# Differential attention first, with plain fp32 scores on row tiles and PV of two units on column tiles

## The chip, the cores and the metric

One core of one Trainium2 chip runs the whole program. The metric is device time in microseconds (us), from launch to the end of the program; the span is the part of it that the profiler sees the engines in. TensorE (PE) multiplies matrices, VectorE (DVE), ScalarE (ACT) and GpSimd (POOL) work on the rest, and SyncE (SP) issues most of the transfers.

## The reference

Two layers of a diffusion trunk on 640 tokens (512 latent ones on a grid of 8 rows of 64, and 128 context ones), width 1024. A layer projects the modulated, normalised tokens once and splits the columns into four groups of 256: three kinds of attention with four heads of 64 each, and a convolution. Their outputs go through one projection, and a feed-forward part of width 4096 follows. The latent tokens also read 128 cached keys.

```
# differential attention: two maps of 32 columns a head, both rotated by rope
p = softmax(q1 @ k1.T * scale) - lam * softmax(q2 @ k2.T * scale)
o_da = rmsnorm(p @ v) * g * (1 - lam_init)
# neighbourhood attention: 8 rows x 16 columns around the token, with a bias, and the context
p = softmax(concat(qg @ kb.T * scale + bias, q @ kc.T * scale)); o_na = p @ v
# latent attention (MLA): 64 + 32 columns a head, queries and keys out of low-rank projections
o_mla = softmax(concat(q_nope, q_rope) @ k_m.T * scale) @ v_m
# convolution over 31 tokens for each channel, layernorm, silu
mixed = concat(o_da, o_mla, o_na, o_conv) @ w_out
x = x + g1 * mixed;  x = x + g2 * (relu(h @ w_ff1)**2 @ w_ff2)
```

## The kernel before

Tokens lie along the free dimension, channels along the 128 partitions. A product of projections is made of three fp32r matmuls (`mm3`, lines 244 to 246): activations and weights are each cut into a high and a low part, and high x high, high x low and low x high are summed. The weights come in granules of 512 KB through a ring; ScalarE rounds the high part (L192) and POOL, or now and then VectorE, subtracts it (L193).

A layer's mixer (`mix`) runs in this order: the convolution's projection; values for neighbourhood and MLA tiles (`in_v`); four column tiles (`mtile`) of queries and keys, at this place those of the neighbourhood heads; the differential values and the rotated key of MLA with its transposes (kr, L582); then `pipeline`, in which 60 units of attention (a head with 128 queries) go through the stages of the string `PROGRAM`, one unit started in each step. "Sa0 ... T2 ... PV3" says that a unit's scores are issued in its own step, the transposes of its probabilities two steps later and the product with the values (PV) three steps later. Units come in three blocks of 20: neighbourhood, differential, MLA. The stages: S is the scores on TensorE, m the maximum on VectorE, x the exponential on ScalarE, sc the scaling (for the differential heads the combine of two maps, L883), T five transposes on TensorE (L686), ev the copy out of PSUM, PV L697, oc the copy or cut of the output. While units run, `plan` puts pieces of projections between them as fillers, each with a first and a last step out of the table `PL`: first `rest()`, the queries and keys of the differential heads and MLA's first projections.

The differential scores before are single-pass: `da_cut` cuts the scaled queries and the keys (32 columns a map) into high and low parts, `da_stack` copies them by DMA (L842, L843) into a stack of four blocks of 32 partitions, and one fp32r matmul over 128 partitions gives the sum of four products (L863 for the 128 context queries, L865 and L866 for 512 and 128 keys). Neighbourhood scores are fp32 matmuls on 64 partitions (L756 to L758). PV multiplies by the 128 columns of two heads, and half of the output is used.

Beside that the 60 taps of the convolution (L423) run on VectorE in the background; behind them POOL adds two channels (L438), in POOL's one queue with the cuts of granules. `rope` is a shuffle and a product on VectorE (L488, L489) and a product and a sum on POOL (L490, L491). The engines take their instructions in the order that a scheduler writes down when the program is built.

PSUM has three slots of 1024 columns for scores and transposes (`slot`) and two banks of 512 (`g`) for pieces and outputs.

Of the kernel before, what the change touches and what calls it, by code (L numbers as in the profile page):

```python
# [16 lines left out]
T = 640  # L17
# [42 lines left out]
DR = 2  # L60
CUT = "DDDDDGDD"
LEADM = (3, 6, 6, 7)
PL = (0, 15, 22, 24, 27, 26, 34, 34, 41, 46, 59, 25, 28, 58, 63, 18, 23)
# [12 lines left out]
CB = "DDDD"  # L76
# [3 lines left out]
PROGRAM = "Sa0 ma0 | T2 ev2 xa0 Sb0 mb0 xb0 sc1 | PV3 oc3 |".split()  # L80


class Builder:
# [347 lines left out]
    def conv_finish(self, l, dst):  # L431
# [23 lines left out]
        r = [self.F("e", 6144, 512), self.A("cr", 0, 128)]  # L455
# [154 lines left out]
    def da_evac(self, l, p, kind):  # L610
        nc = self.nc

        def evac(h, ps):
            t0, t1 = HALF[h]
            dst = self.qk_q("da", p) if kind == "q" else self.qk_k("da", p)
            nl = min(t1, NLAT) - t0
            if t1 > NLAT:
                c0 = 512 if kind == "q" else 640
                nc.scalar.copy(dst[:, c0:c0 + 128], ps[:, nl:t1 - t0])
                if kind == "k":  # L620
                    nc.sync.dma_start(self.d["dak"][l, :, p], dst[:, 640:768])
            self.rope(dst[:, t0:t0 + nl], ps[:, 0:nl], t0, nl)
        return evac
# [23 lines left out]
    def in_mla(self, l):  # L647
# [31 lines left out]
        self.da_cut(0)  # L679
        self.chain(self.da_stacks(0))  # L680
# [13 lines left out]
    def pv(self, u, p, vals):  # L694
        u["o"] = self.g()[:, 0:128]
        for b, v in enumerate(vals):
            self.nc.tensor.matmul(u["o"], v[:, p * 128:p * 128 + 128] if v.shape[1] > 128 else v, u["pt"][:, b * 128:b * 128 + 128],  # L697
                                  start=b == 0, stop=b == len(vals) - 1)

    def o_copy(self, u, h, i, row):  # L700
        r = slice(64 * (h % 2), 64 * (h % 2) + 64)
        self.nc.scalar.copy(row[r, i * 128:i * 128 + 128], u["o"][r])

    def o_split(self, u, h, i):
        r, c = slice(64 * (h % 2), 64 * (h % 2) + 64), slice(i * 128, i * 128 + 128)
        hi, lo = (self.R("ob", off, 2, T)[r, h // 2, c] for off in (0, 5120))
        self.split(hi, lo, u["o"][r], self.nc.vector)
# [22 lines left out]
    def na_bias(self, kind):  # L730
        return self.F("e", 8192 + 1536 * kind, 384)

    def na_bias_load(self, l, h, kind):
        self.nc.sync.dma_start(self.na_bias(kind), self.d["nab"][l, h, kind])

    def na_unit(self, l, h, i, orow):
        nc = self.nc
        p, r0 = h // 2, 64 * (h % 2)
        rows = slice(r0, r0 + 64)
        q = self.qk_q("na", p)[rows, i * 128:i * 128 + 128]  # L740
        k = self.qk_k("na", p)[rows]
        v = self.v("na")
        nk = 128 if i == 4 else 384
        u = {"nb": nk // 128}

        def S():
            sl = self.slot()
            u["s_"], u["t"] = sl[:, 0:nk], sl[:, 640:1024]
            if i == 4:
                nc.tensor.matmul(sl[:, 0:128], q, k[:, 640:768], start=True, stop=True)  # L750
                return
# [3 lines left out]
            pair = k[:, lo:lo + 2 * step].rearrange("p (a b) -> p a b", b=step)[:, ::-1 if prv < nxt else 1, 0:64]  # L755
            nc.tensor.matmul(sl[:, 0:128], q, pair, start=True, stop=True)  # L756
            nc.tensor.matmul(sl[:, 128:256], q, k[:, i * 128:i * 128 + 128], start=True, stop=True)
            nc.tensor.matmul(sl[:, 256:384], q, k[:, 512:640], start=True, stop=True)  # L758

        def mx():  # L760
# [3 lines left out]
            else:  # L764
                kind = (0, 1, 1, 2)[i]
                nc.vector.tensor_tensor_reduce(out=u["s_"], in0=u["s_"], in1=self.na_bias(kind), scale=-1.0,
                                               scalar=3e38, op0=ALU.add, op1=ALU.min, accum_out=m)
                if i != 1 and h < 3:
                    self.na_bias_load(l, h + 1, kind)

        def ex():
            s = u["s"] = self.small()
            u["e"] = self.F("e", 1536 * ((h * 5 + i) % 4), nk)
# [5 lines left out]
            "PV": lambda: self.pv(u, p, [v[:, 5]] if i == 4 else [self.edge(p)[:, i], v[:, i], v[:, 4]]),  # L779
            "oc": lambda: self.o_split(u, h, i),  # L780
        }

    def mla_unit(self, l, h, i, orow):
        nc = self.nc
        q = self.mq[0:96, h, i * 128:i * 128 + 128]
        k = self.mk[0:96, h]
        v = self.v("na")
        nk = 128 if i == 4 else T
        u = {"nb": nk // 128}

# [13 lines left out]
        def ex():  # L804
# [7 lines left out]
            "PV": lambda: self.pv(u, h // 2, [v[:, 5]] if i == 4 else [v[:, j] for j in range(5)]),  # L812
            "oc": lambda: self.o_split(u, h, i),
        }

    def stk(self, mm):
        return self.R("h", 5632 * mm, T), self.R("h", 5632 * mm + 2560, KEYS)

    def da_hl(self):
        return [self.R("h", 22528 + o, n) for o, n in ((0, T), (2560, T), (5120, KEYS), (8192, KEYS))]  # L820

    def da_cut(self, p):
        nc = self.nc
        qh, ql, kh, kl = self.da_hl()
        q, k = self.qk_q("da", p), self.qk_k("da", p)
        nc.scalar.activation(qh, q, AF.Copy, scale=DA_SCALE)
        nc.vector.scalar_tensor_tensor(out=ql, in0=q, scalar=DA_SCALE, in1=qh.bitcast(F32), op0=ALU.mult, op1=ALU.subtract)
        self.split(kh, kl, k)

    def da_stacks(self, p):  # L830
        for par in range(2):
            yield from self.da_stack(p, par)

    def da_stack(self, p, par):
        nc = self.nc
        qh, ql, kh, kl = (a.bitcast(F32) for a in self.da_hl())
        for mm in (2 * par, 2 * par + 1):
            rows = slice(32 * mm, 32 * mm + 32)
            sq, sk = (a.bitcast(F32) for a in self.stk(mm))
            for b in range(4):  # L840
                to = slice(32 * b, 32 * b + 32)
                nc.sync.dma_start(sq[to], (qh, qh, ql, ql)[b][rows])  # L842
                nc.sync.dma_start(sk[to], (kh, kl, kh, kl)[b][rows])  # L843
                if b % 2:
                    yield

    def da_unit(self, l, h, i, orow):
        nc = self.nc
        v = self.v("da")
        st = [self.stk(2 * (h % 2) + c) for c in range(2)]  # L850
        nk = 128 if i == 4 else T
        sq = self.F("sq", 40 * (h // 2 % 2), 5, 2)
        u = {"nb": nk // 128}

        def S(c):
            if c == 0:
                u["sl"] = [self.slot(), self.slot()]
                u["t"] = self.slot()
                u["s"], u["ee"] = self.small(2), [self.etile(nk), self.etile(nk)]
            sl, (q, k) = u["sl"][c], st[c]  # L860
            q = q[:, i * 128:i * 128 + 128]
            if i == 4:
                nc.tensor.matmul(sl[:, 0:128], q, k[:, 640:768], start=True, stop=True)  # L863
            else:
                nc.tensor.matmul(sl[:, 0:512], q, k[:, 0:512], start=True, stop=True)  # L865
                nc.tensor.matmul(sl[:, 512:640], q, k[:, 512:640], start=True, stop=True)  # L866
# [8 lines left out]
        def sc():  # L875
# [12 lines left out]
            "Sa": lambda: S(0), "Sb": lambda: S(1), "ma": lambda: mx(0), "mb": lambda: mx(1),  # L888
# [6 lines left out]
    def pipeline(self, l, hooks):  # L895
# [8 lines left out]
        for t in range(n + depth):  # L904
            if t < n:
                make, h, i = order[t]
                units.append(make(l, h, i, rows[h // 2]))
# [788 lines left out]
```

## Time and profile before

| what | value |
|---|---|
| median of three runs | 1735.49 us (1735.07, 1735.49, 1737.19) |
| the profiled execution | 1735.52 us, its span 1733.6 |
| TensorE | 1664.6 us busy, 96% of the span |
| weight loads | 1570.3 us, 91% |
| VectorE | 1083.0 us, 62% |
| ScalarE | 740.7 us, 43% |
| POOL | 656.5 us, 38% |

Busy time is what an engine spent in instructions; weight loads run beside matmuls. A row of a timeline starts with the time of the first of its instructions, from the span's start, and the busy time of them together; matmuls overlap their neighbours by the filling of the array, so steps are read from start to start.

### The profile page before, as it was taken

Reading aid. Unit: us, or ns where it says so; the run is one execution under the profiler, and the core shown is the slowest. Engines: PE = TensorE matmul, PEld = TensorE weight load, DVE = VectorE, ACT = ScalarE, POOL = GpSimd, SP = SyncE. Lnnn points to the kernel's source line nnn. Section 1 sums busy time; section 2 is a strip of 40 time slices with the busy share of each in tenths; the row PEclk is TensorE's granted clock in tenths of the full one; section 3 lists DMA queues with packets and bytes.
Section 4 is the critical chain, followed back from the end, with each engine's and each line's share of the span. In section 5 each row is a group of like instructions: output and inputs, shape, how many; then the busy total and the mean of one; then the engine's idle time right before and its main releaser. Section 6 shows DMA issues by size and latency. Waiting matters only on the chain. (4 is left out here: it accounts for less than half of the span.)

```text
span 1733.6 us, 29318 instructions
## 1 busy us (share of the span) xinstructions
PE 1664.6 (96%) x11368; PEld 1570.3 (91%) x11368; DVE 1083.0 (62%) x2136; ACT 740.7 (43%) x1655; POOL 656.5 (38%) x527
## 2 busy tenths in 40 slices
PE   7999999999989999999999899999999999999997
PEld 5869988788889999999999888887989999999997
DVE  4772448868988887876377933886784333333335
ACT  4323666756423332222343247776563322332322
POOL 0225533305344455544324364332343333333330
PEclk8999999999989999999999999999999999999999
DMA  9563244202355454443222222430113222222221
GB/s 367 185 202 106 75 110 101 63 14 86 110 160 167 147 158 147 152 153 111 73 71 71 64 86 84 108 88 20 50 39 97 73 74 74 80 79 74 74 62 61
DMA packets 62331, 178.28 MB, mean 103 GB/s; under 512 B 8656, under 2 KB 20048, under 8 KB 62192
## 3 DMA queue, kind: packets, MB, share of 16 engines
q1 hardware_dynamic: 61984, 176.14, 33.0%
q8 instruction: 89, 1.46, 0.3%
q14 instruction: 50, 0.41, 0.1%
q10 hardware_dynamic: 144, 0.13, 0.0%
q0 software_dynamic: 64, 0.14, 0.0%
HBM read 158.52 MB, written 3.83 MB: 94 GB/s over the span
## 5 line engine op out<-in xcount | busy, mean ns | idle before, releaser
L193 POOL TENSOR_TENSOR ra<-fa,ra 128x512 fp32r<-128x512 f32 (+1 forms) x239 | 345.7, 1459 | 545.2 <-ACT ra L192 524.5
L193 POOL TENSOR_TENSOR we<-fa,we 128x512 fp32r<-128x512 f32 x126 | 188.8, 1510 | 275.2 <-ACT we L192 253.5
L1077 DVE TENSOR_TENSOR fr<-fr 128x384 f32<-128x384 f32 (+1 forms) x128 | 103.9, 814 | 273.7 <-ACT or L1076 150.6
L192 ACT CAST ra<-fa 128x512 fp32r<-128x512 f32 (+1 forms) x240 | 147.2, 621 | 255.1 <-PE s L245 163.7
L244 PE MATMUL s<-ra 128*128 128x256 f32 (+2 forms) x600 | 185.4, 309 | 8.3 <-DVE fa L392 7.6
L245 PE MATMUL s<-ra 128*128 128x256 f32 (+2 forms) x600 | 184.3, 307 | 0.0
L246 PE MATMUL s<-ra 128*128 128x256 f32 (+2 forms) x600 | 184.1, 307 | 0.0
L301 DVE CUSTOM_DVE_ANT_0 fa<-fa 128x1024 f32<-128x1024 f32 x112 | 173.2, 1546 | 0.2
L392 DVE SCALAR_TENSOR_TENSOR fa<-s,fa 128x128 f32<-128x128 f32 (+1 forms) x310 | 121.3, 427 | 74.8 <-PE s L246 74.8
L246 PE MATMUL g<-ra 128*128 128x384 f32 (+2 forms) x508 | 158.3, 312 | 8.7 <-POOL ra L193 8.7
L244 PE MATMUL g<-ra 128*128 128x384 f32 (+2 forms) x508 | 162.2, 319 | 2.5 <-DVE bt L1010 1.9
L245 PE MATMUL s<-ra,we 128*128 128x384 f32 (+1 forms) x480 | 152.1, 317 | 12.0 <-DVE ra L370 12.0
L245 PE MATMUL g<-ra 128*128 128x384 f32 (+2 forms) x508 | 157.8, 311 | 0.8 <-POOL ra L193 0.8
L192 ACT CAST we<-fa 128x512 fp32r<-128x512 f32 x132 | 81.2, 620 | 175.2 <-PE s L245 127.9
L246 PE MATMUL s<-ra,we 128*128 128x384 f32 (+1 forms) x480 | 150.1, 313 | 0.0
L244 PE MATMUL s<-ra,we 128*128 128x384 f32 (+1 forms) x480 | 148.8, 314 | 0.8 <-DVE fa L520 0.8
L392 DVE SCALAR_TENSOR_TENSOR fa<-g,fa 128x128 f32<-128x128 f32 (+1 forms) x266 | 109.3, 441 | 40.4 <-PE g L246 39.0
L244 PEld LDWEIGHTS s<-ra 128*128 128x128 f32 x600 | 115.6, 193 | 17.6 <-DVE fa L392 7.9
L423 DVE SCALAR_TENSOR_TENSOR fa<-fa 128x670 f32<-128x670 f32 x120 | 124.1, 1098 | 0.5
L697 PE MATMUL g<-at 128*128 128x128 f32 x848 | 116.9, 277 | 2.8 <-DVE fa L392 1.5
L245 PEld LDWEIGHTS s<-ra 128*128 128x128 f32 x600 | 115.9, 193 | 4.0 <-issue 4.0
L246 PEld LDWEIGHTS s<-ra 128*128 128x128 f32 x600 | 115.8, 193 | 3.6 <-issue 3.6
(299 smaller groups left out, 4484.4 us busy)
## 6 DMA issues: line engine op xcount, KB each, us to landing
fa<-in_wg SPq DMA_DIRECT2D x187, 512.0 KB, 3.6
fa<-in_wmod SPq DMA_DIRECT2D x73, 512.0 KB, 4.2
at<-in_wmod SPq DMA_DIRECT2D x20, 512.0 KB, 6.5
ra<-ra SPq DMA_DIRECT2D x64, 96.0 KB, 2.2
ra<-ra SPq DMA_DIRECT2D x64, 80.0 KB, 2.3
fa<-in_nab SPq DMA_DIRECT2D x24, 192.0 KB, 3.7
fa<-in_xT SPq DMA_DIRECT2D x8, 320.0 KB, 5.9
os<-in_wmod SPq DMA_DIRECT2D x3, 512.0 KB, 10.2
```

The source lines that it names most:

```text
L192: nc.scalar.copy(hi, src)
L193: (lo_eng or nc.gpsimd).tensor_tensor(out=lo, in0=src, in1=hi.bitcast(F32), op=ALU.subtract)
L244: nc.tensor.matmul(out, a[0], b[0], start=start, stop=False)
L245: nc.tensor.matmul(out, a[0], b[1], start=False, stop=False)
L246: nc.tensor.matmul(out, a[1], b[0], start=False, stop=stop)
L301: self.nc.vector.tensor_tensor_reduce(out=self.junk, in0=slot, in1=self.cb[:, v], scale=1.0, scalar=0.0, op0=ALU.mult, op1=ALU.add, accum_ ...
L392: self.mark = nc.vector.scalar_tensor_tensor(out=xs, in0=ps[:, a - t0:b - t0], scalar=self.mod(l, v, which)[:, m:m + 1], in1=xs, op0=ALU.m ...
L423: nc.vector.scalar_tensor_tensor(out=y, in0=g[:, j:j + 670], scalar=dwh[:, c, j:j + 1], in1=y, op0=ALU.mult, op1=ALU.add)
L697: self.nc.tensor.matmul(u["o"], v[:, p * 128:p * 128 + 128] if v.shape[1] > 128 else v, u["pt"][:, b * 128:b * 128 + 128], start=b == 0, s ...
L1077: nc.vector.tensor_tensor(out=r, in0=r, in1=r, op=ALU.mult)
```

## The change

The differential block comes first and the neighbourhood block second, so that the four early column tiles are the differential queries and keys (with rope), and the eight neighbourhood pieces become fillers. Differential scores are plain fp32 matmuls on 32 partitions, straight from the queries (scaled by ScalarE ahead of rope) and keys; the two maps of a head alternate on two row tiles, each into its own slot. The cuts, the stacks and their transfers go. Neighbourhood units come in pairs of two heads whose scores alternate on two 64-row tiles into the two banks of one slot. PV handles two units at once: each multiplies by its own 64 columns, into the upper or the lower 64 partitions of one bank, two steps behind the scores rather than three. One cut serves both outputs. The rows of silu(c) (`c_rows`: 16 transposes, 4 copies) are made in step 41 of layer 0's pipeline rather than in `start`. Buffers, the order of granules, the table `PL` and the places of the bias loads follow.

```
-PROGRAM = "Sa0 ma0 | T2 ev2 xa0 Sb0 mb0 xb0 sc1 | PV3 oc3 |".split()
+PROGRAM = "Sa0 ma0 | T2 ev2 xa0 Sb0 mb0 xb0 sc1 | PV2 oc2 |".split()
...
+            src = ps[:, 0:nl]
+            if kind == "q":
+                src = self.tmp(nl)
+                nc.scalar.activation(src, ps[:, 0:nl], AF.Copy, scale=DA_SCALE)
+            self.rope(dst[:, t0:t0 + nl], src, t0, nl)
...
+    def pv(self, u, vals):
+        pair = [u["mate"], u] if "mate" in u else [u]
+        u["o"] = o = self.g()[:, 0:128]
+        n = len(vals(u))
+        for b in range(n):
+            for c, w in enumerate(pair):
+                nc_out = o[64 * c:64 * c + 64]
+                self.nc.tensor.matmul(nc_out, vals(w)[b], w["pt"][:, b * 128:b * 128 + 128], start=b == 0, stop=b == n - 1)
...
+            for b in range(nk // 128):
+                for c in range(2):
+                    rows = slice(64 * c, 64 * c + 64)
+                    q, k = self.qk_q("na", p)[rows, i * 128:i * 128 + 128], self.qk_k("na", p)[rows]
...
+                    nc.tensor.matmul(sl[:, 512 * c + 128 * b:512 * c + 128 * b + 128], q, k, start=True, stop=True)
...
-        def S(c):
...
-                nc.tensor.matmul(sl[:, 0:512], q, k[:, 0:512], start=True, stop=True)
-                nc.tensor.matmul(sl[:, 512:640], q, k[:, 512:640], start=True, stop=True)
+            for a, b, to in ((640, 768, 0),) if i == 4 else ((0, 512, 0), (512, 640, 512)):
+                for c in range(2):
+                    rows = slice(64 * (h % 2) + 32 * c, 64 * (h % 2) + 32 * c + 32)
+                    nc.tensor.matmul(u["sl"][c][:, to:to + b - a], self.qk_q("da", h // 2)[rows, i * 128:i * 128 + 128],
+                                     self.qk_k("da", h // 2)[rows, a:b], start=True, stop=True)
...
-        order = [(self.na_unit, h, i) for h in range(4) for i in range(5)]
-        order += [(self.da_unit, h, i) for h in range(4) for i in range(5)]
-        order += [(self.mla_unit, h, i) for i in (0, 1, 2, 4, 3) for h in range(4)]
+        order = [(self.da_unit, h, i, i % 2) for h in range(4) for i in range(5)]
+        order += [(self.na_unit, 2 * p + c, i, c) for p in range(2) for i in range(5) for c in range(2)]
+        order += [(self.mla_unit, h, i, h % 2) for i in (0, 1, 2, 4, 3) for h in range(4)]
```

How the order of instructions moves is seen at three places. On TensorE in layer 0, in the differential block: rows of the kernel before, with names as in the program (s are slots, g banks, ra and or activations and weights in parts, at the probabilities, fa other buffers, bt queries and keys).

```order
L865 MATMUL s_67<-ra 128x512
L866 MATMUL s_67<-ra 128x128
L697 MATMUL g_63<-at_81 128x128 x5
L863 MATMUL s_66<-ra 128x128
L244 MATMUL g_64<-or,ra 128x256
L245 MATMUL g_64<-or,ra 128x256
L246 MATMUL g_64<-or,ra 128x256
```

The same block in the changed kernel:

```order
L850 MATMUL s_67<-bt_617 128x512
L850 MATMUL s_65<-bt_617 128x512
L850 MATMUL s_67<-bt_617 128x128
L850 MATMUL s_65<-bt_617 128x128
L688 MATMUL s_66<-fa 128x128 x5
L704 MATMUL g_64<-at_81 64x128
L243 MATMUL g_63<-ra 128x384
L244 MATMUL g_63<-ra 128x384
L245 MATMUL g_63<-ra 128x384
L243 MATMUL g_63<-ra 128x384
L704 MATMUL g_64<-at_81 64x128 x9
L244 MATMUL g_63<-ra 128x384
```

Both maps' scores now stand together, into two slots; ten PV matmuls of two units (64 rows of output each) stand here in two runs, one of them in the middle of a filler piece.

On POOL in layer 1, around the add behind the convolution's taps (128x670), the rows of the kernel before, where 128x512 are halves of granules and 32x256 is the kr rope:

```order
L1174 TENSOR_TENSOR fa<-at_7878 128x64
L193 TENSOR_TENSOR ra<-fa,ra 128x512 x18
L438 TENSOR_TENSOR fa<-fa 128x670
L193 TENSOR_TENSOR ra<-fa,ra 128x512 x4
L490 TENSOR_TENSOR fa<-fa 32x256
```

And of the changed kernel, the last part ahead of the same add (eight, two, two and two cuts stand further ahead, with the rope of the four tiles between them):

```order
L489 TENSOR_TENSOR fa<-fa 128x384
L192 TENSOR_TENSOR ra<-fa,ra 128x512
L490 TENSOR_TENSOR bt_8064<-bt_8064,fa 128x384
L192 TENSOR_TENSOR ra<-fa,ra 128x512
L489 TENSOR_TENSOR fa<-fa 128x128
L490 TENSOR_TENSOR bt_8064<-bt_8064,fa 128x128
L192 TENSOR_TENSOR ra<-fa,ra 128x512 x4
L437 TENSOR_TENSOR fa<-fa 128x670
L192 TENSOR_TENSOR ra<-fa,ra 128x512 x2
L489 TENSOR_TENSOR fa<-fa 32x256
```

Eighteen halves of granules stood ahead of the add since the 128x64 row, now twenty do, and the rope of the differential queries and keys.

On VectorE in layer 1, the taps (128x670) and the first maximum behind them (L766) in the kernel before:

```order
L423 SCALAR_TENSOR_TENSOR fa<-fa 128x670 x60
L766 ISA s_66,fa<-s_66,fa 128x384
L766 ISA fa 128x1
L488 STREAM_SHUFFLE fa<-s_65 32x256
L489 TENSOR_TENSOR fa<-s_65,fa 32x256
```

In the changed kernel, the end of the same stretch, with the first maximum L855:

```order
L422 SCALAR_TENSOR_TENSOR fa<-fa 128x670
L488 TENSOR_TENSOR bt_8064<-s_67,fa 128x128
L422 SCALAR_TENSOR_TENSOR fa<-fa 128x670 x15
L487 STREAM_SHUFFLE fa<-s_67 32x256
L488 TENSOR_TENSOR fa<-s_67,fa 32x256
L487 STREAM_SHUFFLE fa<-s_67 32x256
L488 TENSOR_TENSOR fa<-s_67,fa 32x256
L855 TENSOR_REDUCE fa<-s_65 128x1
```

Eight shuffles and eight products of the four early tiles now stand among the taps, and the kr rope stands ahead of the first maximum.

## Rows read from the trace of the kernel before

**Rows 1.** Windows: length; busy PE, PEld, DVE, ACT, POOL; TensorE clock; DMA share, GB/s.
```profile
155.70:251.70 96.00, 94.85 (x633) 85.82 (x632) 39.34 (x129) 62.03 (x157) 44.30 (x44) 1.00 0.34 94
251.70:338.00 86.30, 79.69 (x551) 71.51 (x550) 76.06 (x159) 62.67 (x158) 34.28 (x40) 1.00 0.36 88
338.00:414.60 76.60, 75.98 (x520) 66.68 (x518) 51.88 (x118) 44.88 (x110) 17.40 (x14) 1.00 0.16 50
987.40:1094.40 107.00, 96.88 (x633) 87.44 (x632) 47.39 (x139) 62.02 (x157) 48.02 (x47) 0.95 0.30 84
```
**Rows 2.** Waits of TensorE in 251.7 to 338, the longest: total, times, longest.
```profile
PE s L686 <- DVE fa L883: 2.0, 3, 0.9
```
**Rows 3.** Timeline, TensorE on the full array in fp32: start, busy, instructions.
```profile
320.78 1.38 PE L697 MATMUL g<-at 128*128 128x128 f32 x10 [0.61 <-ACT fa L939]
321.91 0.90 PE L865 MATMUL s<-ra 128*128 128x512 f32 x2
```
**Rows 4.** Timeline, TensorE around a neighbourhood unit's scores (64 rows of the array).
```profile
227.33 0.33 PE L245 MATMUL g<-ra 128*128 128x384 f32 x1
227.50 0.34 PE L246 MATMUL g<-ra 128*128 128x384 f32 x1
227.77 0.48 PE L756 MATMUL s<-bt 64*128 64x128 f32 x2
...
228.32 0.38 PE L758 MATMUL s<-bt 64*128 64x128 f32 x2
228.63 0.55 PE L686 MATMUL s<-fa 128*128 128x128 f32 x3
229.02 0.39 PE L697 MATMUL g<-at,fa 128*128 128x128 f32 x2
```
**Rows 5.** Timeline, TensorE: column tiles of 2 and 32 columns, and weight loads.
```profile
36.79 0.34 PE L245 MATMUL s<-ra 128*128 128x384 f32 x1
37.06 0.62 PE L1263 MATMUL s<-os,fa 128*2 128x128 f32 x16
37.61 0.45 PE L246 MATMUL s<-ra 128*128 128x384 f32 x1
37.89 0.34 PE L244 MATMUL s<-ra,wes 128*128 128x384 f32 x1
...
73.24 1.06 PE L1358 MATMUL s<-at,fa 128*32 128x512 f32 x8
74.24 0.38 PE L244 MATMUL s<-ra 128*128 128x256 f32 x1
...
78.39 0.95 PE L1366 MATMUL s<-fa 128*128 128x2 f32 x8
79.27 1.25 PE L1358 MATMUL s<-fa 128*32 128x512 f32 x8
```
**Rows 6.** Timeline, TensorE: one map's differential scores, and the filler behind.
```profile
324.71 0.50 PE L865 MATMUL s<-ra 128*128 128x512 f32 x1
...
325.10 0.39 PE L244 MATMUL g<-or,ra 128*128 128x384 f32 x1
```
**Rows 7.** Groups by line: busy, mean ns of one, idle before.
```profile
L870 DVE TENSOR_REDUCE fa<-s 128x1 f32<-128x640 f32 x64 | 51.6, 817 | 4.7 <-PE s L866 2.9 <-ACT fa L702 1.3
L873 ACT ACTIVATE fa<-s,fa 128x640 f32<-128x640 f32 x64 | 51.1, 799 | 19.5 <-DVE fa L870 18.4 <-DVE fa L878 0.8
L488 DVE STREAM_SHUFFLE fa<-g 128x384 f32<-128x384 f32 x8 | 4.8, 596 | 0.4 <-issue 0.4
```
**Rows 8.** Timelines of layer 1's stall: VectorE, POOL, TensorE.
```profile
984.86 10.84 DVE L423 SCALAR_TENSOR_TENSOR fa<-fa 128x670 f32<-128x670 f32 x13
995.78 1.37 POOL L438 TENSOR_TENSOR fa<-fa 128x670 f32<-128x670 f32 x1 [14.04 <-DVE fa L423]
997.11 1.26 POOL L193 TENSOR_TENSOR ra<-fa,ra 128x512 fp32r<-128x512 f32 x1
998.43 0.69 PE L246 MATMUL g<-ra 128*128 128x384 f32 x1 [8.73 <-POOL ra L193]
```

More of the change, by code (lines that the diff above doesn't have):

```diff
@@ L744, in na_unit @@
         u = {"nb": nk // 128}
+        bias = 6 * p + 2 * (0, 1, 1, 2, 0)[i] + h % 2
         def S():
[L747 to L750, printed above, removed]
+            if mate:
+                u["mate"], sl = mate, mate["sl"]
+            else:
+                sl = u["sl"] = self.slot()
+            u["s_"] = u["t"] = sl[:, 512 * (h % 2):512 * (h % 2) + nk]
+            if mate:
                 return
@@ L811, in mla_unit, with da_unit @@
             "ev": lambda: self.turn_out(u),
-            "PV": lambda: self.pv(u, h // 2, [v[:, 5]] if i == 4 else [v[:, j] for j in range(5)]),
-            "oc": lambda: self.o_split(u, h, i),
-        }
[L816 to L847, printed above, removed]
+            "pv": lambda: [v[:, j, 64 * h:64 * h + 64] for j in ([5] if i == 4 else range(5))],
+            "PV": lambda: self.pv(u, lambda w: w["pv"]()), "oc": lambda: self.o_split(u, "ob", h // 2, i), "u": u,
+        }
+    def da_unit(self, l, h, i, orow, mate):
         nc = self.nc
         v = self.v("da")
-        st = [self.stk(2 * (h % 2) + c) for c in range(2)]
         nk = 128 if i == 4 else T
@@ L905, in pipeline @@
             if t < n:
-                make, h, i = order[t]
-                units.append(make(l, h, i, rows[h // 2]))
+                make, h, i, second = order[t]
+                units.append(make(l, h, i, rows[h // 2], units[-1]["u"] if second else None))
+                units[-1]["u"]["pv"] = units[-1]["pv"]
             for p in PROGRAM:
@@ L914, in pipeline @@
                     continue
-                if stage in units[x]:
+                make, h, i, second = order[x]
+                alone = make == self.da_unit and i == 4
+                if stage in units[x] and (second or alone or stage not in ("PV", "oc")):
                     units[x][stage]()
-                make, h, i = order[x]
                 if stage == "oc" and make == self.da_unit and h % 2 == 1 and i == 4:
@@ L1444, in mix @@
                 done, pos, t0, t1, gen, n = job
-                if pos == 0 and t0 == PL[9]:
+                if pos == 0 and t0 in (PL[1][0], PL[3][0]):
                     self.finish_chains("da")
+                if pos == 0 and t0 == PL[1][0]:
+                    for b in range(3):
+                        self.na_bias_load(l, b)
                 pos += 1
```

180 lines of the change are left out of this document (85 added, 95 removed).

## The prediction

> **What bounds the kernel now.** I read a table by stretch first, because only the attention part is changed [rows 1]. In layer 0 it runs from 155.7 (behind the kr transposes) over the neighbourhood and the differential to the end of the MLA stretch at 414.6, 258.9 us. TensorE is busy 94.85 of 96.0 us in the first, 79.69 of 86.3 in the second (with VectorE at 76.06) and 75.98 of 76.6 in the third. So it idles 1.15 + 6.6 + 0.6 = 8.4 us, most of it in the differential stretch, where the list of waits begins with transposes that wait for VectorE's combine of two softmaxes [rows 2]. The rest of the time is TensorE's own, so instructions on it are what I price. In layer 1 the neighbourhood stretch takes 107.0 us, 11.0 more than in layer 0: 8.7 of it is one wait for a weight cut on POOL, which stands behind the convolution's last add, which waits for VectorE's taps [rows 8].
>
> **PV in pairs.** An fp32 matmul of 128 moving columns leaves two records; ten records take 320.78 to 321.91, 0.112 each, so 0.224 a matmul [rows 3]. A layer has 220 PV matmuls: 49.3 us. After, those of two units alternate on two 64-column halves of the array. Counted in the order of the changed kernel they fall into 127 slots (a pair, or a single one where a filler stands between). If the halves run side by side a slot costs 0.224, in all 28.4: **-20.8**. Column tiles in the kernel of before do run so: 16 records on four tiles of 2 columns take 37.06 to 37.61, 0.55 us, where one after the other they would take 1.8; 8 records of 512 columns on four tiles of 32 take 73.24 to 74.24, 1.00, where 8 x 0.45 would be 3.6 [rows 5]. The other bound is no overlap, 0.
>
> The weights speak against the full gain: eight records with two moving columns, little but a weight load each, take 78.39 to 79.27, 0.11 each [rows 5], as long as those of the stream [rows 3]. If each pass of a pair had to pay half a load more, 0.056, a slot would grow by 0.112 and the layer by 14. I take none, because 16 loads fit into the 0.55 us. The Trainium skill, TensorE: Matmul & The Clock Gate, section The mechanism, says that a weight load overlaps a running matmul only when its row group differs, and two column halves share theirs; by that rule some 14 us a layer would be paid, and the 16 records in 0.55 us do not agree with it.
>
> **Neighbourhood scores in pairs.** 52 matmuls at 0.224 become 32 slots of two 64-row tiles: 11.6 to 7.2, **-4.5**. No row shows two row tiles at work at once, so the bounds are -4.5 and 0; I take the first, as the column tiles are the nearest rows.
>
> **Differential scores.** Before, one single-pass fp32r matmul over 128 rows for each map and piece: 0.39 us for 512 + 128 columns [rows 6]; the layer's 72, each with what it costs going in and out, sum to 17.0 from start to start. After, plain fp32 on 32 rows: 512 columns are 4 x 0.224 = 0.90, 128 are 0.22. With the two maps always side by side a layer would be 16 x 1.12 + 4 x 0.22 = 18.8. The order breaks some pairs: of 26 runs 9 hold one tile alone. The longer tile of each run sums to 13184 columns, 103 x 0.224 = 23.1: **+6.1**. One after the other it is 21504 columns, 37.6: +20.6. I take the end by which the column tiles run.
>
> **Going in and out of tiles.** The diff doesn't show this cost. Around one neighbourhood visit of before: the fp32r stream steps 0.17, but 0.27 to the first score; four records take 0.55 (0.45 in the stream), the last two 0.31 (0.22), and the three transposes behind 0.39 (0.34): 0.36 in all [rows 4]. Around the column visit at 37.06: 0.27 and 0.28 for steps of 0.17, and 0.55 for four records' worth (0.45): 0.32 [rows 5]. Before, a layer has 21 visits, 7.6 us. In the order of after I count 92 (47 runs of PV, 26 of differential and 19 of neighbourhood scores), with 21 borders that go straight from one tile mode to the other: 92 x 0.32 - 21 x 0.16 = 26. **+18.4**. The bounds: only the way in, 0.10 a visit, would make it +1.6; 0.36 for every visit +25.5.
>
> **Waits.** The differential stretch takes over the 8 neighbourhood query and key pieces and gets longer on TensorE. From counts in the order, each kind at its duration in the trace, TensorE then has some 120, 60 and 68 us in the differential, neighbourhood and MLA stretches, VectorE 82, 43 and at most 76 (it loses the cuts and gains copies of outputs), ScalarE 85, 55 and 55. So TensorE is the bound in all three, and I give them the idle share of the two stretches that it bounds now (1.75 of 172.6 us), about 3 us: **-5.4**. What covers this: both maps' scores now sit in one visit, and the next unit's wait for a maximum and two exponentials, 0.82 + 0.80 + 0.80 and the hand-overs [rows 7], while the order has 2.9 us or more of TensorE work between visits. Without that cover each of 20 units would wait up to some 0.5 us, and that is late next.
>
> **Smaller.** The stacks' 64 transfers a layer go; nothing waited for them [rows 2]. The rows of silu(c), 16 transposes, move from the start into layer 0: 16 x 0.112 = **+1.8** there; out of the start they save between 0 and 1.8, of which I take 0.2, since that part waits for weights. Bias loads and granules move on SP's queue with their sizes unchanged; the ring of granules ahead of TensorE hides that, and if it didn't, a late bias load would hold a maximum.
>
> **Layer 1.** VectorE is busy with taps to 995.7; then POOL adds (1.37) and cuts (1.26), and TensorE goes on at 998.4 [rows 8]. After, four rope tiles stand among the taps: each a shuffle of 0.60 and a shorter one of 128 columns, which I take as 0.30 [rows 7], with a product as long behind each, so 1.8; four make 7.2. The kr rope, two shuffles and products of 256 columns and another 1.8 by these rows, comes ahead of the first maximum. POOL's add starts 7.2 later, but one granule more is cut ahead of it, worth 4.2 us of TensorE's work, so the stall grows by 3.0, and the late first maximum adds, I estimate, 0.7: **+3.7**. Bounds: 0, if TensorE has enough cut, and +9.0.
>
> **Sum.** Layer 0: -20.8 - 4.5 + 6.1 + 18.4 + 1.8 - 5.4 = -4.4. Layer 1: the same without the 1.8, -6.2, and +3.7: -2.5. Start -0.2. In all -7.1. The profiled execution took 1735.52, 1.9 of it outside its span; the median is 1735.49. So **1728 us**; this case's own range is 1717 to 1734 (visits at 0.26 take 5.5 off a layer, at 0.35 add 3).
>
> **Rivals.**
> A. The borders are cheaper than those shown, because many runs follow other fp32 work: at 0.20 a visit and 0.10 off a direct border they cost 16.3 rather than 26, 19 less in two layers: 1709. Against: the two kinds measured agree within 0.04.
> B. The waits come back: the chain of maximum and exponentials, VectorE's longer queue in layer 1, or ScalarE at 55 of 60 us in the neighbourhood stretch. As much idling as now gives 1728 + 11 = 1739; twice layer 1's stall gives 1739 + 9 = 1748.
> C, on the other side: row tiles don't overlap, or in part. Without overlap the differential scores cost 14.5 more and the neighbourhood's 4.5 more a layer, 1766; half of it gives 1747. It decides from 19% of the overlap lost (7.1 of 38). For it: no row shows two row tiles at work together. Against: the column tiles. The Trainium skill, the same page, section Measured speedup vs the span model, has four row tiles at 3.07 times the speed of one; the same share for two would be 1.54 times, as an estimate some 5.7 us a layer and 1739 in all; no row here shows it.
> D. The pairs of PV pay for their weight loads as above, 14 us a layer: 1756. Against it stand the 16 records in 0.55 us.
> E. No effect: what TensorE saves is given back waiting for weights ahead of the feed-forward part. 1735. Against: the granules wait for TensorE in the attention part, not it for them, but for the one stall.
>
> **How the numbers follow.** Forecast 0.45, A 0.10, B 0.19, C 0.16, D 0.06, E 0.04. A difference of 0.2%, 3.5 us, is about what a measurement can tell from none, so same is 1732 to 1739. Faster: 0.41 of the forecast, A's 0.10, 0.02 of B and C: 0.53. Same: 0.04 of the forecast, 0.06 of B, 0.02 of C, E's 0.04: 0.16. Slower: 0.31. The range leaves out A's lower half, C's upper half and a little of D: 1710 to 1756.
>
> **What would show it.** Right: PV pairs at 0.224, their records starting together; the two maps' L850 within some 0.9 us; borders of 0.3; TensorE idle below 4 us in layer 0's attention; one wait for POOL of 11 to 13 us around 990 to 1005. Wrong: L850's second tile starting as the first ends (C), PV pairs of 0.3 or more (D), or scores and transposes waiting for VectorE or ScalarE in many places (B).

## The result and the profile after

The changed kernel took 1750.74 us (median of four runs, 1746.92 to 1752.20) against 1735.98: a ratio of 1.0081, 95% interval 1.0063 to 1.0099. I had forecast 1728; it is 14.8 us slower instead.

The page of the changed kernel, first part (1664.6, 1570.3, 1083.0, 740.7 and 656.5 us before):

```profile
span 1748.2 us, 29259 instructions
...
PE 1676.8 (96%) x11512; PEld 1532.7 (88%) x11512; DVE 1086.2 (62%) x2113; ACT 719.9 (41%) x1595; POOL 660.2 (38%) x523
```

TensorE is busy 12.2 us longer. Where this and the rest lie is seen by cutting the span at marks that both programs have: the kr transposes of each layer, its last PV matmul, and TensorE's end. All times are lengths between these marks in the timelines, TensorE's idle time in brackets (in the first column without the time ahead of the first matmul, 5.2 and 7.3 us).

| kernel | to kr, layer 0 | to last PV | to kr, layer 1 | to last PV | to the end |
|---|---|---|---|---|---|
| before | 155.7 (6.7) | 259.0 (8.4) | 572.6 (18.6) | 270.4 (17.4) | 468.1 (5.1) |
| changed | 160.3 (9.5) | 258.2 (4.1) | 593.7 (31.0) | 257.1 (4.2) | 471.2 (7.7) |

The attention part itself (second and fourth column) gained 0.8 and 13.3 us; the stretches ahead of it lost 4.6 and 21.1. Without its idle time TensorE works 254.1 and 252.9 us in the attention parts, against 250.6 and 253.0 before, so pairs and fp32 scores together took no work off it. The windows of layer 0's differential, neighbourhood and MLA stretches and of layer 1's differential one, which answer to [rows 1]:

```profile
160.30:282.10 121.80, 120.93 (x815) 97.82 (x812) 71.89 (x148) 76.49 (x183) 46.30 (x53) 1.00 0.17 52
282.10:346.70 64.60, 62.44 (x483) 51.12 (x482) 34.08 (x114) 46.18 (x125) 18.26 (x13) 1.00 0.24 72
346.70:418.50 71.80, 70.70 (x486) 54.09 (x486) 47.58 (x107) 37.36 (x88) 16.07 (x14) 1.00 0.17 53
1012.20:1135.10 122.90, 122.03 (x814) 98.37 (x813) 74.64 (x150) 76.32 (x183) 47.66 (x55) 1.00 0.17 52
```

TensorE is nearly never idle in them, as forecast (4.1 us in layer 0 against 8.4), and the stall that layer 1's attention began with is gone. It stands earlier now. The waits of TensorE from 860 to 1030, where [rows 8] had one wait of 8.73 for POOL:

```profile
PE s L243 <- DVE bt L488: 6.5, 2, 3.8
PE s L245 <- POOL ra L192: 3.0, 1, 3.0
PE s L244 <- POOL ra L192: 3.0, 2, 1.8
```

L243 to L245 are the projection's matmuls. They wait for rope in two ways. One is its product on VectorE (L488): the program gives a bank of PSUM to the next matmuls only when rope has read it. The other is the cuts of granules (L192), which on POOL stand in one queue behind rope's other half. The timelines of VectorE and POOL show what rope waits for:

```profile
980.53 4.93 DVE L422 SCALAR_TENSOR_TENSOR fa<-fa 128x670 f32<-128x670 f32 x3
...
985.39 0.29 DVE L487 STREAM_SHUFFLE fa<-fa 128x128 f32<-128x128 f32 x1
985.59 1.14 DVE L488 TENSOR_TENSOR bt<-fa 128x128 f32<-128x128 f32 x1
986.65 2.92 DVE L422 SCALAR_TENSOR_TENSOR fa<-fa 128x670 f32<-128x670 f32 x3
...
990.79 0.55 DVE L488 TENSOR_TENSOR bt<-s,fa 128x384 f32<-128x384 f32 x1
```

```profile
982.88 3.70 POOL L192 TENSOR_TENSOR ra<-fa,ra 128x512 fp32r<-128x512 f32 x2
986.54 0.50 POOL L489 TENSOR_TENSOR fa<-fa 128x128 f32<-128x128 f32 x1
987.12 0.90 POOL L490 TENSOR_TENSOR bt<-bt,fa 128x128 f32<-128x128 f32 x1
990.15 1.56 POOL L489 TENSOR_TENSOR fa<-fa 128x384 f32<-128x384 f32 x1 [2.13 <-DVE fa L487]
991.68 1.89 POOL L192 TENSOR_TENSOR ra<-fa,ra 128x512 fp32r<-128x512 f32 x1
```

Most rope pieces stand behind three or four taps (128x670) on VectorE, and POOL waits 2.13 us for a shuffle before it can go on to the next cut. Three taps take 4.93 us where POOL is busy for 4.8 us beside them, and 2.92 where it is busy for 1.3. The windows from the first tap to the first maximum in layer 1 tell the size, the first of the changed kernel and the second of the kernel before:

```profile
937.80:1016.60 78.80, 66.30 (x439) 64.14 (x438) 78.48 (x91) 17.21 (x42) 47.87 (x34) 0.91 0.27 78
```

```profile
931.50:995.60 64.10, 58.19 (x426) 57.39 (x424) 64.10 (x61) 18.29 (x44) 26.20 (x14) 0.97 0.29 84
```

VectorE is full in both. It has 78.5 us of work ahead of the first maximum rather than 64.1: 8.8 more for rope, and 5.9 more for the same 60 taps (70.0 from start to start rather than 64.1), since POOL is busy 47.9 us rather than 26.2 beside them. And with TensorE's waits its granted clock falls: 0.91 in the mean of the window, rather than 0.97. Of the 21.1 us that layer 1 lost ahead of its attention part, 12.4 are idle time (31.0 rather than 18.6). By the clocks of the two windows the slower clock costs some 5 more (an estimate: 0.09 of 78.8 us rather than 0.03 of 64.1).

### The profile page after: what moved, and what is told of

Same layout as the page of the kernel before. It is cut to its first block, busy times and chain, and to the rows that moved or that the text cites. A ratio compares the mean times of both kernels' runs of the same rounds, so it can differ in the third digit from the quotient of the medians.

```text
span 1748.2 us, 29259 instructions
## 1 busy us (share of the span) xinstructions
PE 1676.8 (96%) x11512; PEld 1532.7 (88%) x11512; DVE 1086.2 (62%) x2113; ACT 719.9 (41%) x1595; POOL 660.2 (38%) x523
## 3 DMA queue, kind: packets, MB, share of 16 engines
HBM read 158.52 MB, written 3.83 MB: 93 GB/s over the span
## 5 line engine op out<-in xcount | busy, mean ns | idle before, releaser
L192 POOL TENSOR_TENSOR ra<-fa,ra 128x512 fp32r<-128x512 f32 (+1 forms) x239 | 352.2, 1487 | 483.1 <-ACT ra L191 453.0
L192 POOL TENSOR_TENSOR we<-fa,we 128x512 fp32r<-128x512 f32 x126 | 190.1, 1520 | 312.3 <-ACT we L191 254.7
L191 ACT CAST ra<-fa 128x512 fp32r<-128x512 f32 x240 | 146.8, 622 | 301.4 <-PE s L244 171.5
L243 PE MATMUL s<-ra 128*128 128x256 f32 (+2 forms) x592 | 185.9, 314 | 16.4 <-DVE bt L488 9.4
L245 PE MATMUL s<-ra 128*128 128x256 f32 (+2 forms) x592 | 183.5, 310 | 3.0 <-POOL ra L192 3.0
L243 PE MATMUL g<-ra 128*128 128x384 f32 (+2 forms) x516 | 164.8, 319 | 0.0
L244 PE MATMUL g<-ra 128*128 128x384 f32 (+2 forms) x516 | 160.8, 312 | 0.8 <-POOL ra L192 0.8
L245 PE MATMUL g<-ra 128*128 128x384 f32 (+2 forms) x516 | 159.9, 310 | 0.0
L243 PE MATMUL s<-ra,we 128*128 128x384 f32 (+1 forms) x472 | 148.1, 316 | 2.7 <-ACT ra L378 1.7
L245 PE MATMUL s<-ra,we 128*128 128x384 f32 (+1 forms) x472 | 148.4, 315 | 0.0
L243 PEld LDWEIGHTS s<-ra 128*128 128x128 f32 x592 | 115.6, 195 | 27.9 <-issue 10.7
L422 DVE SCALAR_TENSOR_TENSOR fa<-fa 128x670 f32<-128x670 f32 x120 | 137.9, 1199 | 0.7
L245 PEld LDWEIGHTS s<-ra 128*128 128x128 f32 x592 | 115.6, 195 | 4.6 <-POOL ra L192 3.3
L243 PE MATMUL g<-or,ra 128*128 128x384 f32 (+1 forms) x318 | 108.3, 341 | 2.2 <-DVE fa L391 1.0
```

What stands on the lines that cost most here:

```text
L191: nc.scalar.copy(hi, src)
L192: (lo_eng or nc.gpsimd).tensor_tensor(out=lo, in0=src, in1=hi.bitcast(F32), op=ALU.subtract)
L243: nc.tensor.matmul(out, a[0], b[0], start=start, stop=False)
L244: nc.tensor.matmul(out, a[0], b[1], start=False, stop=False)
L245: nc.tensor.matmul(out, a[1], b[0], start=False, stop=stop)
L422: nc.vector.scalar_tensor_tensor(out=y, in0=g[:, j:j + 670], scalar=dwh[:, c, j:j + 1], in1=y, op0=ALU.mult, op1=ALU.add)
```

## The experiments

Theory W after the result: the loss is VectorE's work ahead of the first maximum, to which rope was added among the taps, with what queues behind it. Rival P: TensorE's own work in the attention part (borders of tiles, fp32 scores), and the stretches ahead only show it moved. Each run was timed in three rounds beside the kernel before, 1736.0 to 1736.4 in its four groups.

**Taps cut short, in both kernels.** This takes VectorE's load away and leaves TensorE's order as it is; most of the convolution is left out.

```
-            nc.vector.scalar_tensor_tensor(out=y, in0=g[:, j:j + 670], scalar=dwh[:, c, j:j + 1],
-                                           in1=y, op0=ALU.mult, op1=ALU.add)
+            nc.vector.scalar_tensor_tensor(out=y[:, 0:8], in0=g[:, j:j + 8], scalar=dwh[:, c, j:j + 1],
+                                           in1=y[:, 0:8], op0=ALU.mult, op1=ALU.add)
```

> The changed kernel with each of the 60 taps of a layer's convolution cut to 8 of its 670 columns (the convolution's output is left out; TensorE's order of instructions stays the same). Theory W, the four early column tiles wait for rope on VectorE behind the taps and for cuts on POOL behind rope: the 5.9 us in layer 0 and 18.5 us in layer 1 ahead of the attention part go, about 1726 us, and within 3 us of the kernel before with taps cut in the same way. Rival P, TensorE's own work in the attention part (borders of tiles, fp32 scores) makes the loss: at most the 11 us of the stall that before had go as well, about 1739, 10 or more above the kernel before so cut.

> The kernel before with the same cut of the taps to 8 columns (the convolution's output is left out). Both theories: the stall of 8.7 us in layer 1 and its slow clock behind it go, 1735.5 - 11 = 1724.5, 1720 to 1728. Its distance to the changed kernel with short taps is what tells W (under 3 us) from P (10 or more).

Measured: 1724.58 us (ratio 0.9933, 0.9919 to 0.9948) for the changed kernel and 1725.29 (0.9938, 0.9923 to 0.9953) for the one before. The 14.8 us are gone. Of TensorE's waits between 850 and 1030 in the changed kernel with short taps these are left:

```profile
PE s L244 <- DVE ra L369: 2.2, 2, 1.2
PE s L243 <- DVE fa L519: 0.8, 1, 0.8
PE g L244 <- POOL ra L192: 0.8, 1, 0.8
```

W holds, P falls. The attention parts keep their lengths (258.3 and 256.2 us, table below), so they were not what moved. Taps cost the changed kernel 26.2 us and the kernel before 10.7. In layer 0, from the last modulation matmul of the start (L1250; L1271 in the kernel before) to kr, the changed kernel takes 99.8 us with short taps rather than 106.8, and the kernel before 100.6 rather than 101.0.

**PV on the whole array** in the changed kernel.

```
-        for b in range(n):
-            for c, w in enumerate(pair):
-                nc_out = o[64 * c:64 * c + 64]
-                self.nc.tensor.matmul(nc_out, vals(w)[b], w["pt"][:, b * 128:b * 128 + 128], start=b == 0, stop=b == n - 1)
+        for c, w in enumerate(pair):
+            for b in range(n):
+                self.nc.tensor.matmul(u["o"][c], vals(w)[b], w["pt"][:, b * 128:b * 128 + 128], start=b == 0, stop=b == n - 1)
...
-            "pv": lambda: [v[:, j, 64 * h:64 * h + 64] for j in ([5] if i == 4 else range(5))],
+            "pv": lambda: [v[:, j, h // 2 * 128:h // 2 * 128 + 128] for j in ([5] if i == 4 else range(5))],
...
```

> The changed kernel with PV on the whole array again: each unit multiplies by the 128 columns of two heads, into its own 128 columns of a bank; the cut runs on two halves. If pairs of column tiles run side by side (my step): 220 x 0.224 = 49.3 rather than 28.3 us a layer, +21, less some 35 to 47 visits of 0.29 (-13), so +7 to +8 a layer, about 1765. Rival, pairs bring nothing net, because the borders eat it: 1747 to 1754.

Measured: 1771.98 us (1.0211, 1.0193 to 1.0228), the attention parts 11.3 and 12.5 us longer. The pairs of PV are worth 21 us net to this kernel; column tiles do run side by side.

**Fewer visits to tiles**, in two ways: PV three steps behind (in that kernel the probabilities of a pair's first unit are overwritten before use, so its time is that of the same work on other numbers), and the two halves issued in the other order.

```
-PROGRAM = "Sa0 ma0 | T2 ev2 xa0 Sb0 mb0 xb0 sc1 | PV2 oc2 |".split()
+PROGRAM = "Sa0 ma0 | T2 ev2 xa0 Sb0 mb0 xb0 sc1 | PV3 oc3 |".split()
```

```
-            for c, w in enumerate(pair):
+            for c, w in reversed(list(enumerate(pair))):
```

> The changed kernel with PV and its output three steps behind the scores, as before, rather than two. In the order the visits to tiles fall from 92 to 78 a layer and the PV slots from 127 to 113: 14 x 0.29 + 14 x 0.22 = 7 us a layer, 1737 in all if borders and single halves cost what the trace shows. Rival, these are covered or a later PV makes new waits: 1748 to 1753.

> The changed kernel with the two halves of a PV pair issued in the other order, the later unit first, so that a run no longer starts before the second unit's probabilities are there. In the order the visits to tiles fall from 92 to 77 a layer and lone halves from 34 to 4 (15 slots fewer). If each visit costs 0.29 and each slot 0.22, it is 7.7 us a layer less, 1735; with PV three steps behind, a like saving of 14 brought 9.5, so 1735 to 1741. Rival, waits take it back: 1746 to 1752.

Measured: 1741.27 (1.0029, 1.0019 to 1.0040) and 1745.53 (1.0064, 1.0042 to 1.0085). The first brought 9.5 of the 14 us expected, the second 5.2 of 15. In the second, TensorE's work in layer 0's attention fell by 5.7 us and its idle time there rose by 3.6. The forecast of 7.7 a layer overrated it: more than half of the work that was avoided came back as waits.

**Three ways around the rope.** Keys copied out of PSUM by ScalarE; rope's other half on VectorE; taps later.

```
+            src = self.tmp(nl)
+            nc.scalar.activation(src, ps[:, 0:nl], AF.Copy, scale=DA_SCALE if kind == "q" else 1.0)
```

```
-        nc.gpsimd.tensor_tensor(out=sh, in0=sh, in1=self.sinT[rows, t0:t0 + n], op=ALU.mult)
-        nc.gpsimd.tensor_tensor(out=dst, in0=dst, in1=sh, op=ALU.add)
+        eng.tensor_tensor(out=sh, in0=sh, in1=self.sinT[rows, t0:t0 + n], op=ALU.mult)
+        eng.tensor_tensor(out=dst, in0=dst, in1=sh, op=ALU.add)
```

```
-DR = 2
+DR = 7
...
-            nc.vector.tensor_reduce(out=u["m", c], in_=u["sl"][c][:, 0:nk], axis=AX.X, op=ALU.max, negate=True)
+            self.mark = nc.vector.tensor_reduce(out=u["m", c], in_=u["sl"][c][:, 0:nk], axis=AX.X, op=ALU.max, negate=True)
...
-            self.tick(RATE[0])
+            self.tick(self.rt[0])
...
+        self.rt = ((2700,1000,700), (1600,700,500))[l]
```

In the last, `rt` sets how many taps are issued beside each piece, and `DR` the pipeline step by which all of them are.

> The changed kernel with the differential keys copied out of PSUM by ScalarE ahead of rope, as the queries are, so that a bank of PSUM no longer waits for VectorE. If it is the banks that hold TensorE up (9.4 us of waits for the product of rope): about 1741, and a faster clock behind it. If it is VectorE's total ahead of the first maximum, and POOL's cuts behind rope: 1747 to 1753, the waits turn up at other places.

> The changed kernel with all four steps of rope for the differential queries and keys on VectorE, none on POOL. VectorE gets 4 x 1.4 = 5.6 us a layer more; POOL loses some 16 us a layer. If VectorE's own work alone counts: 5 us a layer later, 1756 to 1760. If a tap's 1.65 us beside a busy POOL against 0.83 beside an idle one counts too (16 us of POOL are then worth 8 us of VectorE), and cuts that queue behind rope: 1738 to 1747.

> The changed kernel with 13 (layer 0) and 24 (layer 1) of the 60 taps issued behind the first maxima of the attention part instead of ahead of them; nothing is left out. Theory W, VectorE's work ahead of the first maximum makes the loss: the first maximum of layer 1 comes some 25 us earlier, the waits of TensorE ahead of the attention part go, less 3 to 5 us a layer for maxima that now wait behind a tap: 1728 to 1738. Rival P, the loss is TensorE's own work: 1746 or more.

Measured: 1751.89 (1.0093, 1.0078 to 1.0109), 1748.27 (1.0081, 1.0062 to 1.0100) and 1746.05 (1.0059, 1.0041 to 1.0077). With the copy, the banks no longer hold TensorE up, but from 850 to 1035 it waits for this:

```profile
PE s L244 <- POOL ra L192: 5.0, 3, 3.0
PE s L848 <- ACT fa L856: 4.8, 1, 4.8
PE s L245 <- POOL ra L192: 3.2, 1, 3.2
```

L848 is the second unit's scores, L856 an exponential behind the first maximum, which came at 1015.1 rather than 1016.6: the stretch ahead is 5.5 us shorter and layer 1's attention 7.8 longer. Moving the wait doesn't shorten VectorE's line. With all of rope on VectorE the taps of layer 1 took 66.3 us rather than 70.0, but the rope 15.4 rather than 8.8; the time is the same within the spread of both kernels. With late taps the stretches ahead lost 6.0 and 9.5 us and the attention parts grew by 7.8 and 3.7, because maxima and combines then wait behind taps. In all it gained 4.7 us, where W foresaw 13 to 23: the waits ahead of the attention part shrink, but most of that comes back in it. (There the convolution ends later than in the program's plan of its buffers, so part of its output is overwritten.)

**The pairs alone, on the kernel before**; then with the fp32 row-tile scores too (in that kernel MLA's keys take the place of the differential queries and keys while these are in use, so the numbers differ, not the work); then the pairs without the differential block, and that with late taps.

```
+        order = [(self.na_unit, 2 * p + c, i, c) for p in range(2) for i in range(5) for c in range(2)]
+        order += [(self.da_unit, h, i, i % 2) for h in range(4) for i in range(5)]
+        order += [(self.mla_unit, h, i, h % 2) for i in (0, 1, 2, 4, 3) for h in range(4)]
...
+            for c, w in reversed(list(enumerate(pair))):
```

> The kernel before with only the pairs of the change: PV of two units on two column halves (later unit first), neighbourhood scores of two heads on two row tiles, one cut for both outputs; the neighbourhood block stays first, the differential scores stay on the stacks. By the order 51 visits to tiles a layer and 112 PV slots: 28.3 - 49.3 for PV and 3.5 more for fewer lone slots, -4.3 for neighbourhood scores, 51 x 0.29 - 8.1 = +7 for visits: TensorE 22 us a layer less. If all of it counts 1692; if VectorE bounds the differential stretch as before (76 of 86 us) and part returns as waits, as 40% did with the other order of PV, 1705 to 1718. Rival, what made the changed kernel slow lies in the pairs: 1730 or more.

> As the kernel with only the pairs, and the differential scores on 32-row tiles in plain fp32 too, without cuts and stacks; the block order stays that of before, so that no rope stands ahead of the attention part. Scores of 25.8 and 37 visits x 0.29 = 10.7 rather than 17.0, +19 a layer on TensorE; VectorE loses the cuts. If TensorE bounds, 20 to 38 us above the kernel with only the pairs; if VectorE bounded the differential stretch there, 0 to 15 above it.

> The kernel before with pairs for the neighbourhood and MLA units alone (scores of two heads, PV of two units); the differential units keep stacks, full-array PV and three steps. In the kernel with pairs everywhere the neighbourhood stretch took 89.4 rather than 96.0 us, the MLA stretch 76.6 rather than 76.7, the differential one 92.4 rather than 86.4 with 14.1 us of idling on TensorE. If it is the pairing in the differential stretch that couples units and makes it wait: 86.4 again, 6.6 a layer less from the neighbourhood block and 0 to 5 from MLA: 1712 to 1723. Rival, any shortening of TensorE's work is given back: 1732 to 1740.

> The same with some 23 of layer 1's 60 taps issued behind the first maxima of the neighbourhood block, where VectorE is busy 42 of 89 us; nothing is left out. If VectorE's work ahead of the first maximum is what holds layer 1 up, the wait of 8.3 us for POOL goes and the half clock behind it: 8 to 11 us below the kernel without late taps, 1702 to 1714. Rival, taps among the maxima cost as much as they save: within 3 us of it.

Measured: 1739.95 (1.0024, 1.0013 to 1.0036), 1764.43 (1.0157, 1.0134 to 1.0180), 1750.08 (1.0076, 1.0058 to 1.0094) and 1754.79 (1.0093, 1.0068 to 1.0118): three misses; only the second came out as expected, 24.5 us above the first. The first was expected at 1705 to 1718, the third at 1712 to 1723 and the fourth at 1702 to 1714. By its number the first falls to its rival, that the pairs made the changed kernel slow; but in the changed kernel PV's pairs save 21 us, so they are not what made it slow. The page and the waits of the differential stretch of the kernel with pairs (its traced execution took 1735.73, the shortest of ten):

```profile
PE 1639.2 (95%) x11368; PEld 1518.2 (88%) x11368; DVE 1084.5 (63%) x2116; ACT 725.1 (42%) x1595; POOL 656.4 (38%) x527
```

```profile
PE s L883 <- ACT fa L891: 5.1, 4, 1.7
PE s L686 <- DVE fa L901: 4.7, 5, 1.8
PE g L702 <- ACT at L692: 1.4, 3, 0.8
```

TensorE's busy time fell by 25.4 us and none of it was gained. In layer 0 its idle time rose from 8.4 to 20.9, 14.1 of it in the differential stretch: scores (L883) wait for an exponential, transposes (L686) for VectorE's combine of two maps (L901). The granted clock fell as well. Layer 0's differential stretch with pairs, with row scores too, and with pairs but for the differential block (in [rows 1] it has 79.69 us of 86.3 and a clock of 1.00):

```profile
246.00:338.40 92.40, 78.26 (x529) 65.36 (x527) 76.21 (x155) 58.82 (x144) 33.64 (x38) 0.93 0.35 86
242.10:358.20 116.10, 112.00 (x655) 79.56 (x655) 80.87 (x170) 61.93 (x155) 31.36 (x39) 0.91 0.11 31
246.70:349.50 102.80, 89.99 (x583) 79.65 (x582) 78.10 (x166) 63.34 (x161) 35.51 (x41) 0.91 0.33 79
```

So in the kernel before that stretch stands close to its chain of maximum, exponential and combine, and time taken off TensorE alone returns in two ways: as waits, 7.5 us more in the first line, and as a slower clock, some 6 by an estimate (0.07 of 92.4 us). The kernel with pairs outside the differential block got that block 16.5 us longer (third line): 6.2 are idle time (12.8 rather than 6.6), and the clock makes some 9 by the same estimate. With late taps the 8.3 us wait for POOL did go, but 5.2 us of waits for rope's product (L489) took its place.

The fp32 scores on top cost 12.6 and 15.5 us in the two attention parts, with TensorE's idle time down to 8.9 and 16.8; part of it is clock, as the second line shows. That kernel is nearly the change without its new order of blocks, and it is 13.7 us slower than the changed kernel (1750.74). So the order that put rope among the taps gave back more than it cost. The changed kernel's differential stretch ran at a granted clock of 1.00, with 0.9 us of idle time in 121.8; this one at 0.91, with 4.1 in 116.1. Why the clock differs, and what else the order gave, is not shown.

The same marks for all runs:

| kernel | to kr, layer 0 | to last PV | to kr, layer 1 | to last PV | to the end |
|---|---|---|---|---|---|
| changed, short taps | 156.0 | 258.3 | 572.3 | 256.2 | 470.8 |
| before, short taps | 157.8 | 259.2 | 571.1 | 261.2 | 467.6 |
| changed, PV whole | 159.4 | 269.5 | 591.6 | 269.6 | 471.2 |
| changed, PV three steps | 161.3 | 253.6 | 591.6 | 253.9 | 471.9 |
| changed, PV order | 161.5 | 256.1 | 593.5 | 253.9 | 470.8 |
| changed, keys copied | 159.0 | 258.4 | 588.2 | 264.9 | 470.8 |
| changed, rope on VectorE | 159.7 | 258.3 | 584.6 | 264.3 | 471.3 |
| changed, late taps | 154.3 | 266.0 | 584.2 | 260.8 | 471.2 |
| before, pairs | 156.6 | 258.4 | 572.4 | 267.3 | 471.3 |
| before, pairs and row scores | 158.9 | 271.0 | 573.6 | 282.8 | 472.3 |
| before, pairs but differential | 156.2 | 265.6 | 571.9 | 274.4 | 471.1 |
| the same, late taps | 157.8 | 271.9 | 571.9 | 273.7 | 472.0 |

No version that was run is faster than the kernel before with its whole work.

## Why the prediction was wrong

**The steps that failed** are two: the one on layer 1, "+3.7", together with its silence on layer 0, and the sizes in the attention part. The runs with short taps split the miss. Forecast and result, -7.1 and +14.8, lie 21.9 us apart. Taps cost the changed kernel 15.5 us more than the kernel before, where the forecast had 3.7: 11.8 of them. Without taps the kernels differ by -0.7, where the forecast without its 3.7 gives -10.8: the other 10.1.

**Taps and rope.** The step on layer 1 placed the added rope on VectorE ahead of the first maximum, which was right, with 9.0 us for it where 8.8 were measured, and then let the four column tiles run through at TensorE's own pace, so that only the later start of POOL's add counted. What the runs showed: the tiles themselves run at VectorE's pace, because a bank of PSUM is handed back by rope's product and a granule is cut on POOL behind rope's sums; each of both waits for a shuffle behind taps. Ahead of the attention part this cost 18.5 us in layer 1 (21.1 less the 2.6 that layer 0's last projection came later) in place of a stall of 11.0 (14.7 with the 3.7), and in layer 0, where I had nothing, 5.9 (4.6 with 1.3 saved at the start). With short taps both are gone (99.8 against 100.6 us in layer 0, and in layer 1 only waits are left that the kernel before has too), which shows that the taps make them. Of the two waits the copied keys took the first away and gained nothing, so it is VectorE's queue as a whole that sets the pace, not the bank alone. I had read the order's rope rows among the taps, and counted them as VectorE's time only; that POOL's half slows the taps (5.9 us) was left out as well.

**Sizes in the attention part.** I forecast -4.4 and -6.2 a layer without the stall. With short taps the two kernels differ by -0.9 and -5.0 up to the last PV, but 1.2 and 3.2 us come back behind it: +0.3 and -1.8. So some 4.5 us a layer were lacking. From start-to-start sums over layer 0's rows: PV's 260 steps 28.3 us (forecast 28.4), neighbourhood scores 7.0 (7.2), 92 visits some 27.1 (26) against 8.1 before (7.6): all nearly as priced. Differential scores are 25.8 rather than 23.1, 2.7 more: I take it that the two maps' records pair up less often than the count by columns assumes, which no run tests. TensorE idles 4.1 us, not 3, 1.1 more; the visits, less those of before, add 0.6. These make 4.4.

**Rivals.** A (cheap borders) is refuted: 27.1 us for 92 visits, 0.29 each. E (no effect) is refuted by the interval. C is refuted by the timelines, in which the records of two tiles start 6 or 7 ns apart. One differential unit, one neighbourhood pair and one PV pair with what follows each:

```profile
242.99 1.35 PE L850 MATMUL s<-bt 32*128 32x512 f32 x8
244.27 0.76 PE L688 MATMUL s<-fa 128*128 128x128 f32 x5
```

```profile
293.97 1.18 PE L774 MATMUL s<-bt 64*128 64x128 f32 x12
295.07 0.44 PE L243 MATMUL g<-ra 128*128 128x384 f32 x1
...
298.31 0.88 PE L704 MATMUL g<-at 128*64 128x128 f32 x12
299.11 0.44 PE L243 MATMUL g<-ra 128*128 128x384 f32 x1
```

Eight fp32 records of two maps, 512 and 128 columns, take 1.28 us from start to start, where one map alone needs 1.12 by the rates of [rows 3]; the rest is the border. The twelve records of the neighbourhood pair take 1.10 with their borders, where one after the other at 0.112 they would take 1.34 without. Twelve PV records take 0.80, six slots of 0.112 and a border. D falls with this. By the Trainium skill, TensorE: Matmul & The Clock Gate, section The mechanism, a weight load overlaps a running matmul only when its row group differs; these pairs of column halves share theirs, and the 0.80 us leave no room for such a wait, so the trace does not agree. B is the nearest to what happened: it named VectorE's longer queue in layer 1, and 1748 for twice its stall. But its waits belonged to the attention part, where there is less idle time than before (4.1 and 4.2 us); they came ahead of it, and in layer 0 too. That the result lies near 1748 is in part luck, as 10.1 us of the miss come from the attention part's sizes.

## What to carry to other kernels

When a piece of work is moved to an earlier place, price the engine that evacuates it, not only the one that computes it: who frees its bank, and what stands in front of that instruction on its queue. Time taken off one engine is only worth what the other engines' chain leaves free at that place: PV's pairs were worth 21 us where TensorE was the bound, and pairs brought nothing where the chain of maximum, exponential and combine stood close behind. Read the granted clock of a stretch before its busy time: waits there came with a clock of 0.93 and 0.91, which took part of what the shorter work had saved. To tell a moved wait from a cost, cut the suspected load in both kernels and compare the two.

## What the runs showed of the hardware

A tap on VectorE (two operands in SBUF) steps 0.84 us beside an idle POOL and 1.6 beside a busy one (means of 25 and 18 taps in layer 1 of the changed kernel). A product of rope shows the same: 1.14 us when it reads its source from SBUF beside POOL's cut (at 985.59), and 0.28 for the same 128 columns out of PSUM, beside POOL's work too:

```profile
997.47 0.28 DVE L488 TENSOR_TENSOR bt<-s,fa 128x128 f32<-128x128 f32 x1
```

```profile
996.80 1.06 POOL L489 TENSOR_TENSOR fa<-fa 128x128 f32<-128x128 f32 x1
```

The Trainium skill, SBUF — State Buffer, section Who interferes with whom, states that a VectorE instruction with two SBUF inputs contends with a GpSimd instruction that reads SBUF; the 1.6 us against 0.84 and the 1.14 against 0.28 agree. So a copy from PSUM to SBUF ahead of such a product, made to free a bank early, puts the product among the instructions that a busy POOL holds up: with the keys copied the ten products of layer 1 took 6.3 us from start to start rather than 5.2.

TensorE's granted clock fell in the stall: 0.51 from 990 to 995, close to the lower of its two levels (1.2 rather than 2.4 GHz), behind waits of 1.17 and 3.83 us. Steps of the 128x288 matmuls then were 0.24 us rather than 0.13:

```profile
987.01 0.29 PE L243 MATMUL s<-ra 128*128 128x288 f32 x1
987.14 0.29 PE L244 MATMUL s<-ra 128*128 128x288 f32 x1
987.27 0.30 PE L245 MATMUL s<-ra 128*128 128x288 f32 x1
991.39 0.61 PE L243 MATMUL s<-ra 128*128 128x288 f32 x1 [3.83 <-DVE bt L488]
...
992.04 0.44 PE L245 MATMUL s<-ra 128*128 128x288 f32 x1
992.28 0.44 PE L243 MATMUL s<-ra 128*128 128x288 f32 x1
```

So a wait of TensorE can cost more than its length: in layer 0 of the changed kernel one wait of 2.95 us for rope stands in a stretch that became 5.9 us longer, with a granted clock of 0.66 from 140 to 150.
